# Hybrid gMLP and state-space layer: where the first scalings of the second projection stand on VectorE, and the order of its weight places

## The chip, the cores and the metric

The kernel runs on one core of a Trainium2 chip. A core has a matrix engine (PE), a vector engine (DVE), a scalar engine (ACT), GpSimd (POOL) and SyncE (SP), which here only sends DMAs. Each engine takes its instructions in order, and waits for the others through semaphores. The metric is the device time of one execution in microseconds.

## The reference

One layer on 1024 tokens of width 1024, in float32. The parts around the change:

```
proj = h @ w_in                       # 11296 columns: u, v, z of the gMLP; z, x, B, C, dt of the state space; two gates
y_a = spatial_gating(gelu(gm_u), gelu(gm_v), ...) * silu(gm_z)
y_b = ssd_scan(xh, dt, a, bm, cm)     # 8 groups x 8 chunks of 128 tokens, state carried from chunk to chunk
y_b = y_b + xh * d_skip[:, None]
yz  = (y_b * silu(ssm_z)).reshape(b, s, 8, 256)
y_b = rms_norm(yz, ssm_norm_w)        # root mean square over each group's 256 channels
merged = sigmoid(g_a) * (y_a @ w_proj_a) + sigmoid(g_b) * (y_b @ w_proj_b)
x = x + gate * (merged @ w_out)       # and a last rms_norm over the row
```

## The kernel before

Every large product is made with float32r matmuls of a high and a low part of each operand: high x high, high x low and low x high, three matmuls of 128x128 by 128x512. The kernel has four stages in a row on PE: the input projection; the state-space stage; the second projection, y_b @ w_proj_b; and the output projection.

**The state-space stage** has 32 steps, (group, pair of chunks), written (g,s), in pairs of groups; the last four are (6,2), (7,2), (6,3) and (7,3). A step has three parts. `prep` makes products and transposes on PE (`pc`, `px`); DVE multiplies the decay matrix `dcy` with `pc` (L1183) and scales the transposed input into `xd` and `xe` (L1186). `front` multiplies them (`yi`, and `sp` for the state); DVE adds `sp` to the state `st` (L1236) and forms `y` (L1216). `back` multiplies the state (`yn` in PSUM, eight matmuls of which the last four need the new `st`), DVE scales that by `ea` into `ym` (L1262), and POOL makes y + ym (L1264) and y times z (L1265), which is `yz`. ACT stores `yz` to `yb_d` in device memory. For the root mean square ACT squares `yz` (L1289; for the last halves, `lq`, L1281), POOL adds the two squares (L1293, L1285), PE sums over channels (`pq`), DVE copies that to `cwt` or `tri` (L1305), and it goes through `ms_d` to POOL's power (L1320) and as `rs_d` back to memory. Between the steps PE is filled with matmuls of the first projection, `pma`, which DVE scales into `tha` (L1526) and ACT stores to `mt_d`.

Within this stage each engine's order is written out: `link(key, f)` makes the instructions of `f` stand behind the last linked one of that engine. What is not linked is placed by the scheduler at build time, by its own priorities.

**The second projection** has 56 units, (product, k) for seven products of 2x2 blocks and eight slices of 128 channels, each of twelve matmuls of 128x512; the first product is `p1` (`x0p` to `x3p`). `loads(u)` runs six units ahead and sends, on SP, the tile `rb` (the inverse roots, one for two slices), the row tile `yn` (slice n and half h of y_b from `yb_d`) and the weights: for `p1` raw ones, `p1r`, 128x512. `operands(u)` runs four units ahead: DVE scales `yn` by weight and `rb` (`y_norm`, L1653), ACT and DVE split it into `p1bh` and `p1bl` (L1691, L1692), and the raw weights into `p1a` (L1698, L1699). The first of these loads and operands are issued while the state-space stage still runs. (The name `yn` is used twice: PE's result in `back`, and these row tiles.)

The raw weights of `p1`, and later the gate tiles `tg` and `ma` and `junk`, lie in places that the state-space stage leaves: three each of `xd` and `xe`, two of `ea`. `gate_slot` deals them out in a fixed order of eight. SP's queue is in order too: a load whose place is not yet free holds all loads behind it. All DMAs of SP and ACT share eight semaphores in rotation (DMAHW0 to 7), and each waits until the one before it on its semaphore has landed.

Of the kernel before, what the change touches and what calls it, by code (L numbers as in the profile page):

```python
# [12 lines left out]
ALU = mybir.AluOpType  # L13
# [22 lines left out]
def hybrid_kernel(  # L36
# [7 lines left out]
    V, A, G, PE = nc.vector, nc.scalar, nc.gpsimd, nc.tensor  # L44
# [85 lines left out]
    snw = par2[:, 32:48]  # L130
# [980 lines left out]
    def link(key, f):  # L1111
        if key in last:
            with tc.issue_after(last[key]):
                i = f()
        else:
            i = f()
        last[key] = i.ins
        return i
# [330 lines left out]
    p2r = ps1 = psum = None  # L1449
# [9 lines left out]
    for n, (name, _, _, d1, d2, g) in enumerate(todo):  # L1459
# [11 lines left out]
        if n == len(jobs):  # L1471
# [6 lines left out]
            p2r = p2rpool.__enter__()  # L1478
# [4 lines left out]
        if n + 2 == len(todo):  # L1483
            wspool.__exit__(None, None, None)
            p2xpool = tc.tile_pool(name="p2x", bufs=1, side="right", reuse_waits="tile")
            p2x = p2xpool.__enter__()
# [132 lines left out]
    def slot_tile(name, dt=F32):  # L1619
        tag = room.pop(0)  # L1620
        t = hp.tile([P, 512], dt, name=name, tag=tag)
        tags_of[name] = tag
        return t
# [4 lines left out]
    n_gate = [0]  # L1628

    def gate_slot(name):  # L1630
        n_gate[0] += 1
        pool, tag, b = ((p2x, "xd", 3), (p2x, "xe", 3), (p2r, "ea", 2), (p2x, "xd", 3), (p2x, "xe", 3), (p2x, "xd", 3),
                        (p2x, "xe", 3), (p2r, "ea", 2))[n_gate[0] % 8]
        return pool.tile([P, 512], F32, name=name, tag=tag, bufs=b)


# [4 lines left out]
    yt, rbs = {}, {}  # L1641
# [8 lines left out]

    def y_norm(n, h):
        t = yt[n, h]
        V.scalar_tensor_tensor(t, t, snw[:, n : n + 1], rbs[n // 2, h], op0=ALU.mult, op1=ALU.mult)  # L1653

    units = [(nm, k) for nm in ("p1", "p3", "p6", "p5", "p7", "p2", "p4") for k in range(KT)]
    aops, bops, raws = {}, {}, {}
# [3 lines left out]
    def loads(u):  # L1660

        nm, k = units[u]
        if nm in fresh:
            n, h = fresh[nm]
            y_load(n + k, h)
        aops[u] = t = big(f"{nm}a{k}", F32R).rearrange("p (v c) -> p v c", v=2)
        if nm in WB:
            load(f32(t), wb_d[k][:, WB[nm]])
        else:
            raws[u] = raw = gate_slot(f"{nm}r{k}") if nm == "p1" else slot_tile(f"{nm}r{k}")  # L1670
            n = k if nm == "p1" else KT + k
            load(raw, w_proj_b[n * P : (n + 1) * P, 0:512])

    def operands(u):

        nm, k = units[u]
        if nm in fresh:
            n, h = fresh[nm]
            y_norm(n + k, h)
# [43 lines left out]
    def gate_load(b, h):  # L1723
        hs = slice(h * 512, (h + 1) * 512)
        th, ma = gate_slot(f"tg{b}_{h}"), gate_slot(f"ma{b}_{h}")
        load(th, th_d[(KT + b) * P : (KT + b + 1) * P, hs])
        load(ma, mt_d[b][:, hs])
        gates[b, h] = th, ma
# [109 lines left out]
    for u, (nm, k) in enumerate(units):  # L1838
# [28 lines left out]
        if k == KT - 1:  # L1867
            for j in range(4):
                with tc.high_priority():
                    if nm in ("p1", "p3", "p5"):  # L1870
                        t = slot_tile(f"{nm}_{j}")
# [80 lines left out]
    SPLITS = {"a11": ("t1",), "s1": ("t2",), "s2": ("t3",), "s3": ("t4", "b22"), "a22": ("b21",)}  # L1952
    acc = {"x": banks("ox", "y"), "y": banks("oy", "x")}
    junk = gate_slot("junk")
    for nm, bn, pn, first, t0, c, done in PRODUCTS:
        ps = acc[pn]
# [112 lines left out]
```

## Time and profile before

| | us |
|---|---|
| median of 3 runs | 1365.01 (1363.45 to 1365.26) |
| profiled execution | 1364.88 |
| its span, first to last instruction | 1362.9 |
| PE busy | 1348.8 |
| DVE busy | 1056.7 |
| ACT busy | 800.2 |
| POOL busy | 195.6 |

The profile shows one execution; times in its rows are us from the start of the span. A row of a timeline gives start, duration, engine, line, operation and tiles, the number of instructions that it merges, and in brackets how long the engine had been idle before and what ended that. The profiled execution's own time is 2.0 us longer than the span.

### The profile page before, as it was taken

How to read it: one execution, taken by the hardware profiler on the slowest of the kernel's cores; microseconds unless marked ns; L12 is line 12 of the kernel's file. 1: busy time of each engine (PE TensorE's matmuls, PEld its weight loads, DVE VectorE, ACT ScalarE, POOL GpSimd, SP SyncE). 2: the span in 40 equal slices, each digit the busy share in tenths (PEclk: the TensorE clock that was granted, in tenths of full speed). 3: DMA queues.
4: the chain of work that ended last, by engine and by line, in shares of the span. 5: the costliest groups of instructions: out<-in, count | busy, mean ns of one | idle time of the engine just before them, and what ended most of it. 6: DMA issues, size and time to landing. Idle time of an engine off the chain costs nothing. (4 is left out here: it accounts for less than half of the span.)

```text
span 1362.9 us, 20106 instructions
## 1 busy us (share of the span) xinstructions
PE 1348.8 (99%) x6907; PEld 1115.4 (82%) x6907; DVE 1056.7 (78%) x1731; ACT 800.2 (59%) x1446; POOL 195.6 (14%) x193
## 2 busy tenths in 40 slices
PE   8999999999999999999999999999999999999997
PEld 6688888888888888888888888888888878888886
DVE  4786886787777898688887788458888867959976
ACT  4754666666657665466576655486877734233453
POOL 1000000000000000000000000007898971000002
PEclk9999999999999999999999999999999999999999
DMA  9675444333345667777656866489889868978913
GB/s 284 184 247 140 136 124 124 117 119 121 101 132 155 193 185 230 245 217 245 204 193 192 245 203 185 158 295 307 304 294 315 303 235 289 318 261 319 377 50 124
DMA packets 249577, 288.64 MB, mean 212 GB/s; under 512 B 16860, under 2 KB 196484, under 8 KB 249476
## 3 DMA queue, kind: packets, MB, share of 16 engines
q1 hardware_dynamic: 174868, 203.80, 46.9%
q10 hardware_dynamic: 74544, 83.57, 17.9%
q8 instruction: 54, 0.88, 0.3%
q14 instruction: 47, 0.39, 0.1%
q0 software_dynamic: 64, 0.00, 0.0%
HBM read 199.82 MB, written 87.49 MB: 211 GB/s over the span
## 5 line engine op out<-in xcount | busy, mean ns | idle before, releaser
L1159 POOL TENSOR_SCALAR_AFFINE_SELECT dcy<-dcy 128x1024 f32<-128x1024 f32 x32 | 35.3, 1103 | 787.9 <-DMA yl<-ya_d 744.6
L1167 ACT ACTIVATE dcy<-dcy,nacs 128x128 f32<-128x128 f32 x256 | 78.3, 389 | 2.9 <-POOL dcy L1159 2.3
L1265 POOL TENSOR_TENSOR yz<-y,sl 128x512 f32<-128x512 f32 x32 | 44.7, 1396 | 2.5
L1183 DVE TENSOR_TENSOR dcy<-dcy,pc 128x1024 f32<-128x1024 f32 x32 | 39.0, 1219 | 7.5 <-PE pc L85 5.9
L82 PE MATMUL pma<-yh,wah 128*128 128x512 f32 x128 | 43.1, 418 | 0.0
L82 PE MATMUL pma<-yh,wal 128*128 128x512 f32 x128 | 42.5, 413 | 0.0
L1190 ACT COPY bn<-pc 128x256 f32<-128x256 f32 x32 | 11.9, 371 | 49.6 <-DVE dcy L1183 48.7
L1653 DVE SCALAR_TENSOR_TENSOR yn<-yn,par,rb 128x512 f32<-128x512 f32 x32 | 25.6, 801 | 19.5 <-DMA yn<-yb_d 19.5
L82 PE MATMUL pma<-yl,wah 128*128 128x512 f32 x128 | 40.2, 395 | 0.0
L1155 ACT ACTIVATE ea<-dcy 64x512 f32<-64x512 f32 x64 | 39.8, 622 | 0.4
L1060 ACT ACTIVATE ac<-ac 128x1024 f32<-128x1024 f32 x32 | 34.0, 1061 | 9.2 <-DVE ac L1058 9.0
L1264 POOL TENSOR_TENSOR y<-y,ym 128x512 f32<-128x512 f32 (+1 forms) x32 | 37.0, 1156 | 7.1 <-DVE ym L1262 7.1
L1058 DVE SCALAR_TENSOR_TENSOR ac<-c2x,cwt,ac 128x1023 f32<-128x1023 f32 (+2 forms) x24 | 30.7, 1280 | 8.8 <-ACT ac L1056 8.7
L1058 DVE SCALAR_TENSOR_TENSOR ac<-c2cb,cwt,ac 128x1023 f32<-128x1023 f32 (+2 forms) x24 | 30.7, 1279 | 8.1 <-ACT ac L1056 8.0
L1925 POOL TENSOR_TENSOR r<-r,fnw 128x512 f32<-128x512 f32 x4 | 6.1, 1528 | 206.9 <-ACT junk L1923 206.9
L82 PE MATMUL yi<-dcy,xd 128*64 128x128 f32 x512 | 35.0, 279 | 0.0
L82 PEld LDWEIGHTS yn<-sl,st 128*128 128x128 f32 x224 | 29.8, 191 | 4.0 <-DVE st L1236 1.2
L82 PE MATMUL sp<-xe,bn 128*128 128x256 f32 x112 | 32.7, 409 | 0.0
L82 PEld LDWEIGHTS yi<-dcy,xd 128*64 128x64 f32 x512 | 27.3, 136 | 5.7 <-issue 2.9
L1058 DVE SCALAR_TENSOR_TENSOR ac<-c1cb,cwt,ac 128x1023 f32<-128x1023 f32 (+2 forms) x24 | 30.6, 1277 | 1.3 <-ACT ac L1056 1.3
L82 PE MATMUL yn<-sl,st 128*128 128x128 f32 x224 | 30.5, 275 | 1.0 <-DVE st L1236 1.0
L1022 ACT ACTIVATE vm<-vm,vr 128x128 f32<-128x128 f32 x64 | 25.6, 483 | 9.5 <-DMA vm<-v_d 9.0
(2983 smaller groups left out, 4363.7 us busy)
## 6 DMA issues: line engine op xcount, KB each, us to landing
sl<-s_d SPq DMA_DIRECT2D x32, 768.0 KB, 6.6
s_d<-ac ACTq DMA_DIRECT2D x32, 512.0 KB, 3.3
wb_d<-wbb ACTq DMA_DIRECT2D x32, 512.0 KB, 3.8
dcy<-acs_d SPq DMA_DIRECT2D x32, 512.0 KB, 4.6
av<-in_w_in_dram SPq DMA_DIRECT2D x36, 256.0 KB, 3.3
aw<-in_ada_w_dram SPq DMA_DIRECT2D x16, 512.0 KB, 5.2
wbr<-in_w_proj_b_dram SPq DMA_DIRECT2D x32, 256.0 KB, 4.7
yb_d<-yz ACTq DMA_DIRECT2D x32, 256.0 KB, 5.6
```

What stands on the lines that cost most here:

```text
L82: pin(PE.matmul(acc, l, r, start=first, stop=last))
L1022: A.activation(vn[:, cs], vn[:, cs], AF.Identity, scale=vr[:, 1, ch : ch + 1], bias=vr[:, 2, ch : ch + 1])
L1058: V.scalar_tensor_tensor(ac[:, s:], cc[:, : S - s], conv_wt[:, 3 - s, i : i + 1], ac[:, s:], op0=ALU.mult, op1=ALU.add)
L1060: A.activation(ac, ac, AF.Silu)
L1155: link("A", lambda: A.activation(ea[hh * HD : (hh + 1) * HD], dcy.rearrange("p (j e) i l -> p e j (i l)", e=2)[hh * HD : (hh + 1) * HD, hh ...
L1159: link("G", lambda: G.affine_select(out=d8, in_=d8, compare_op=ALU.is_ge, fill=-1e30, base=0, pattern=[[0, 2 * HPG], [1, P]], channel_mult ...
L1167: link("A", lambda: A.activation(dcy[:, h, i, :], dcy[:, h, i, :], AF.Exp, bias=sub[:, i, h : h + 1]))
L1183: link("V", lambda: V.tensor_tensor(d3, d3, pc[:, 0:256].unsqueeze(1).to_broadcast([P, HPG, 256]), op=ALU.mult))
L1190: link("A", lambda: A.copy(bn, pc[:, 256:512]))
L1264: link("G", lambda: G.tensor_add(y1[:, :, t0:], y1[:, :, t0:], m[:, :, t0:]))
L1265: link("G", lambda: G.tensor_mul(yz, y1, sl[:, 4:6]))
L1653: V.scalar_tensor_tensor(t, t, snw[:, n : n + 1], rbs[n // 2, h], op0=ALU.mult, op1=ALU.mult)
```

## The change

Two edits. The scalings of the first four row tiles (n < 4, first half) are linked: they stand on DVE behind the last linked instruction of the state-space stage. And `gate_slot` deals the eight places in another order: counted from the first call, xe, ea, xd, xe, xd, xe, ea, xd before, and xe, xd, xe, xd, xe, xd, ea, ea now.

```
     def gate_slot(name):
         n_gate[0] += 1
-        pool, tag, b = ((p2x, "xd", 3), (p2x, "xe", 3), (p2r, "ea", 2), (p2x, "xd", 3), (p2x, "xe", 3), (p2x, "xd", 3),
-                        (p2x, "xe", 3), (p2r, "ea", 2))[n_gate[0] % 8]
+        pool, tag, b = ((p2r, "ea", 2), (p2x, "xe", 3), (p2x, "xd", 3), (p2x, "xe", 3), (p2x, "xd", 3), (p2x, "xe", 3),
+                        (p2x, "xd", 3), (p2r, "ea", 2))[n_gate[0] % 8]
...
     def y_norm(n, h):
         t = yt[n, h]
-        V.scalar_tensor_tensor(t, t, snw[:, n : n + 1], rbs[n // 2, h], op0=ALU.mult, op1=ALU.mult)
+        f = lambda: V.scalar_tensor_tensor(t, t, snw[:, n : n + 1], rbs[n // 2, h], op0=ALU.mult, op1=ALU.mult)
+        if n < 4 and h == 0:
+            link("V", f)
+        else:
+            f()
```

PE's, POOL's and SP's instructions stand in the same order as before. DVE at the end of the state-space stage (the first numbers in a name are group and pair of chunks, or the row tile and its half):

```order
 L1216 SCALAR_TENSOR_TENSOR y17_2_10717<-sl7_2_10373,dskt_151,yi7_2_10703 128x256 x2
 L1236 TENSOR_TENSOR st22_8261<-st22_8261,sp7_2_10712 128x256
-L1653 SCALAR_TENSOR_TENSOR yn0_0_10925<-yn0_0_10925,par2_147,rb0_0_10923 128x512
 L1262 TENSOR_TENSOR ym7_2_10749<-yn7_2_10743,ea7_2_10375 128x512
 L1183 TENSOR_TENSOR dcy7_3_10526<-dcy7_3_10526,pc7_3_10754 128x1024
```

The scaling of row tile 0 no longer stands ahead of step (7,2)'s `ym`. Some rows on, still DVE:

```order
-L1653 SCALAR_TENSOR_TENSOR yn1_0_10930<-yn1_0_10930,par2_147,rb0_0_10923 128x512
 L1262 TENSOR_TENSOR ym6_3_10804<-yn6_3_10799,ea6_3_10456 128x512
 L1236 TENSOR_TENSOR st_8258<-st_8258,sp7_3_10819 128x256
 L1216 SCALAR_TENSOR_TENSOR y17_3_10822<-sl7_3_10528,dskt_151,yi7_3_10810 128x256 x2
+L1262 TENSOR_TENSOR ym7_3_10841<-yn7_3_10836,ea7_3_10530 128x512
+L1653 SCALAR_TENSOR_TENSOR yn0_0_10925<-yn0_0_10925,par2_147,rb0_0_10923 128x512
+L1653 SCALAR_TENSOR_TENSOR yn1_0_10930<-yn1_0_10930,par2_147,rb0_0_10923 128x512
 L1653 SCALAR_TENSOR_TENSOR yn2_0_10937<-yn2_0_10937,par2_147,rb2_0_10935 128x512
-L1262 TENSOR_TENSOR ym7_3_10841<-yn7_3_10836,ea7_3_10530 128x512
 L1526 SCALAR_TENSOR_TENSOR tha6_0_10575<-tha6_0_10575,pma6_0_10577 128x512
```

Step (7,3)'s `ym` now stands ahead of the scalings of row tiles 0, 1 and 2, which come together behind it; that of row tile 3 stands one `tha` later. Behind these, DVE's copy of pq(6,1) to `cwt` (L1305) moves from behind the first `p1bl` and `p1a` to ahead of them.

SP's loads of the second projection, before, with the semaphores that each waits for:

```order
L91 DMA p1r1_10933<-in_w_proj_b_dram 128x512 [waits DMAHW4_49,DVE_49,Activation_49]
L91 DMA rb2_0_10935<-rs_d1_59 128x512 [waits DMAHW5_49]
L91 DMA yn2_0_10937<-yb_d2_93 128x512 [waits DMAHW7_49]
L91 DMA p1r2_10940<-in_w_proj_b_dram 128x512 [waits DMAHW0_49]
L91 DMA yn3_0_10949<-yb_d3_94 128x512 [waits DMAHW1_49]
L91 DMA p1r3_10952<-in_w_proj_b_dram 128x512 [waits DMAHW2_49,PE_49]
```

And now:

```order
L91 DMA p1r1_10933<-in_w_proj_b_dram 128x512 [waits DMAHW4_49]
L91 DMA rb2_0_10935<-rs_d1_59 128x512 [waits DMAHW5_49,DVE_49,Activation_49]
L91 DMA yn2_0_10937<-yb_d2_93 128x512 [waits DMAHW6_49]
L91 DMA p1r2_10940<-in_w_proj_b_dram 128x512 [waits DMAHW7_49,DVE_49,PE_49]
L91 DMA yn3_0_10949<-yb_d3_94 128x512 [waits DMAHW0_49,Activation_49]
L91 DMA p1r3_10952<-in_w_proj_b_dram 128x512 [waits DMAHW1_49]
```

`p1r1` had a place of `ea`, and its waits for DVE and ACT were for step (6,3)'s `ym` and `ea`; it now has a place of `xd` that step (7,2) left, and waits only for an earlier DMA. The waits of `rb2` are for step (6,2); `p1r2` waits for `sp` of step (6,3).

## The prediction

> **What bounds the kernel now.** I read the page first (span, busy time of each engine), then the list of PE's waits, then how busy PE is in the stretch behind the change, and last the timelines of PE, VectorE (DVE), POOL, SyncE's queue (SPq) and ScalarE (ACT) around it.
>
> ```profile
> span 1362.9 us, 20106 instructions
> ...
> PE 1348.8 (99%) x6907; PEld 1115.4 (82%) x6907; DVE 1056.7 (78%) x1731; ACT 800.2 (59%) x1446; POOL 195.6 (14%) x193
> ...
> PE yn L82 <- DVE st L1236: 1.0, 1, 1.0
> PE pq L82 <- POOL yz L1293: 0.9, 1, 0.9
> ...
> 1127.00:1350.00 223.00, 222.97 (x984) 184.37 (x983) 183.72 (x301) 84.99 (x160) 10.34 (x8) 1.00 0.71 254
> ```
>
> PE works 99% of the span, so the time can only fall by what PE waits. Two of its few waits lie at the end of the state-space stage, where the change is. From 1127 to 1350 PE is busy for 222.97 of 223.00 us at a granted clock of 1.00: what PE gains before 1127 is carried to the end, as long as its operands come that much sooner too.
>
> PE around the two waits (start, us, work, count; in brackets the idle time before):
>
> ```profile
> 1099.99 1.05 PE L82 MATMUL yn<-sl,st 128*128 128x128 f32 x8
> 1100.88 0.39 PE L82 MATMUL pc<-sl 128*128 128x128 f32 x2
> ...
> 1101.65 0.27 PE L85 MATMUL pc<-ident,sl 128*128 128x128 f32 x1
> ...
> 1103.10 0.70 PE L82 MATMUL sp<-xe,bn 128*128 128x256 f32 x2
> ...
> 1105.48 0.60 PE L82 MATMUL yn<-sl,st 128*128 128x128 f32 x4
> 1107.07 0.71 PE L82 MATMUL yn<-sl,st 128*128 128x128 f32 x4 [0.98 <-DVE st L1236]
> 1107.71 1.09 PE L82 MATMUL yi<-dcy,xd 128*64 128x128 f32 x16
> ...
> 1111.59 1.05 PE L82 MATMUL yn<-sl,st 128*128 128x128 f32 x8
> 1112.40 0.71 PE L82 MATMUL pma<-yh,wal 128*128 128x512 f32 x2
> ...
> 1113.49 0.43 PE L82 MATMUL pq<-yz,ones 128*32 128x128 f32 x8
> 1114.82 0.43 PE L82 MATMUL pq<-yz,ones 128*32 128x128 f32 x8 [0.90 <-POOL yz L1293]
> 1115.18 0.73 PE L82 MATMUL pma<-yl,wah 128*128 128x512 f32 x2
> ...
> 1122.21 0.42 PE L82 MATMUL pq<-lq,ones 128*32 128x128 f32 x8
> ...
> 1125.06 0.42 PE L82 MATMUL pq<-lq,ones 128*32 128x128 f32 x8
> ...
> 1126.91 0.39 PE L1718 MATMUL x0p<-p1bh,p1a 128*128 128x512 f32 x1
> ```
>
> The first wait costs more than its bracket: eight yn matmuls take 0.81 us from start to next start when undisturbed (1111.59 to 1112.40), here 2.23 (1105.48 to 1107.71). The difference is 1.42, or 1.34 against the yn group at 1099.99, which takes 0.89 (0.11 a matmul) when state-space work follows (1100.88), as it does here; I take 1.35. The second is 1114.82 - 1113.49 less the 0.36 that such a group takes (1114.82 to 1115.18): 0.97.
>
> Why DVE and POOL are late there:
>
> ```profile
> 1103.01 0.75 DVE L1653 SCALAR_TENSOR_TENSOR yn<-yn,par,rb 128x512 f32<-128x512 f32 x1 [3.48 <-DMA yn<-yb_d]
> 1103.68 0.68 DVE L1262 TENSOR_TENSOR ym<-yn,ea 128x512 f32<-128x512 f32 x1
> 1104.28 1.21 DVE L1183 TENSOR_TENSOR dcy<-dcy,pc 128x1024 f32<-128x1024 f32 x1
> ...
> 1106.61 0.41 DVE L1236 TENSOR_TENSOR st<-st,sp 128x256 f32<-128x256 f32 x1
> ...
> 1107.72 1.71 DVE L1653 SCALAR_TENSOR_TENSOR yn<-yn,par,rb 128x512 f32<-128x512 f32 x1
> ...
> 1116.15 0.75 DVE L1653 SCALAR_TENSOR_TENSOR yn<-yn,par,rb 128x512 f32<-128x512 f32 x1 [5.02 <-DMA yn<-yb_d]
> 1116.82 0.68 DVE L1262 TENSOR_TENSOR ym<-yn,ea 128x512 f32<-128x512 f32 x1
> ...
> 1124.03 1.38 DVE L1692 TENSOR_TENSOR p1bl<-yn,p1bh 128x512 fp32r<-128x512 f32 x1 [0.72 <-ACT p1bh L1691]
> 1125.33 0.68 DVE L1699 TENSOR_TENSOR p1a<-p1r,p1a 128x512 fp32r<-128x512 f32 x1
> ```
> ```profile
> 1099.61 1.64 POOL L1320 TENSOR_TENSOR ssq<-ssq,nhalf 128x8 f32<-128x8 f32 x1
> 1104.44 1.29 POOL L1264 TENSOR_TENSOR y<-y,ym 128x512 f32<-128x512 f32 x1 [3.19 <-DVE ym L1262]
> ...
> 1107.61 1.27 POOL L1293 TENSOR_TENSOR yz<-yz 128x512 f32<-128x512 f32 x1
> 1108.84 2.10 POOL L1320 TENSOR_TENSOR ssq<-ssq,nhalf 128x8 f32<-128x8 f32 x1
> 1110.90 1.28 POOL L1264 TENSOR_TENSOR y<-y,ym 128x512 f32<-128x512 f32 x1
> ...
> 1113.51 1.26 POOL L1293 TENSOR_TENSOR yz<-yz 128x512 f32<-128x512 f32 x1
> ...
> 1123.57 1.29 POOL L1285 TENSOR_TENSOR lq<-lq,lq 128x512 f32<-128x512 f32 x1 [1.74 <-ACT lq L1281]
> ```
> ```profile
> 1097.21 0.42 SPq L91 DMA_DIRECT2D yn<-yb_d  x1
> ...
> 1110.09 0.33 SPq L91 DMA_DIRECT2D p1r<-in_w_proj_b_dram  x1
> ...
> 1110.95 0.42 SPq L91 DMA_DIRECT2D yn<-yb_d  x1
> ...
> 1122.34 1.15 ACT L1281 ACTIVATE lq<-yz 128x512 f32<-128x512 f32 x2 [5.19 <-DMA mt_d<-tha]
> ```
>
> DVE runs in order. The scaling of row 0 stands ahead of step (7,2)'s ym and waits 3.48 us for its load; ym, dcy, xd, xe and st behind it are late, and PE waits for st. The same ym starts POOL's chain late (3.19 idle), which then runs without a break to the sum at 1113.51, and PE waits for that one. Later the scaling of row 2 waits 5.02 us ahead of step (7,3)'s ym, because SPq sent its load only at 1110.95, behind p1r1, whose place was free only after step (6,3)'s ym.
>
> **The change part by part.** No work is added or removed: the same 32 scalings, the same loads. Four scalings move on DVE, and p1r1 to p1r7 change places.
>
> *Scalings, first wait.* Without the scaling ahead, ym of (7,2) starts when PE's group of 1099.99 ends, about 1101.07. dcy then needs the transposes of 1101.65: it starts at 1102.0 instead of 1104.28, and st 2.33 us behind it as now (1106.61 - 1104.28), at 1104.33. Its input sp ends at 1103.80, so nothing holds it. st ends at 1104.74; PE needs it at 1105.48 + 4 x 0.11 = 1105.92. Margin 1.2 us: the whole 1.35 goes.
>
> *Scalings, second wait.* POOL's first y starts at 1101.83 instead of 1104.44, and its rows keep their distances: the power at 1108.84 - 2.61 = 1106.23, done by 1107.87 with the 1.64 of the row at 1099.61 (1108.33 with the 2.10 here). ym of (6,3) is ready by 1107.2. From the next y to the end of the sum are 3.87 us (1110.90 to 1114.77): 1111.74 to 1112.20. PE comes there at 1113.49 - 1.35 + 0.36 = 1112.50. The 0.97 goes too, with 0.3 to 0.8 us in hand.
>
> *Places.* p1r1 no longer waits for (6,3)'s ym, so SPq goes on at about 1098.7. The loads of rb2 and row 2 are then sent some 11 us sooner; at the 5.8 us from send to use of row 0 (1097.21 to 1103.01) they land near 1106, well before DVE reaches them at 1111.9. p1r2 to p1r5 now wait for matmuls of (6,3) and (7,3), p1r6 and p1r7 for the last ea's; these are needed much later. The gate tiles that use the same eight places later still come eight slots apart. By itself all this costs and brings nothing on PE; it removes the 5.02 us of DVE.
>
> *What is late next.* PE then wants everything from 1115 on 2.32 us sooner: the sums lq by 1119.89 and 1122.74, x0p's operands from 1124.59. ym of (7,3) starts at PE's 1111.59 - 1.35 + 1.08 = 1111.32 instead of 1116.82, 5.5 us sooner, and POOL's last y with it. But now three scalings (0.75 each) stand between it and tha, cwt and tri, on which ACT's in-order queue hangs ahead of lq. The bounds: if DVE runs them unhindered, tri is done at 1116.8, ACT squares lq at 1117.4 and the last sum ends near 1120. If each scaling takes turns with a POOL row, 1.29 + 0.55 us a turn, tri comes at 1119.1, lq's squares (1.15) at 1120.2 and the sum ends at 1122.6. Both are before 1122.74. x0p's third matmul needs p1a's low part, which ends at 1126.01 for a use at 1127.37 now; it is wanted by 1125.05 and, behind lq in ACT, comes between 1122 and 1124.7. So I book nothing here, with 0.2 to 3 us of cover.
>
> *Sum.* 1.35 + 0.97 = 2.32 us off the profiled execution's 1364.88 gives 1362.56. That execution lies 0.13 below the median of 1365.01, so by that it would be 1362.7; with the lowest run at 1363.45 the median stands at the high end, and I say **1362.6**. The bounds of the gain: 1.9 by the brackets alone (0.98 + 0.90), 2.4 with 1.42 for the first.
>
> **Rivals.**
>
> *DVE and POOL take turns, and it costs PE.* The scaling at 1107.72 took 1.71 us instead of 0.75: it ended at 1109.43, 0.55 behind the end of POOL's row at 1107.61 (1108.88), and POOL's next one took 2.10 instead of 1.64. So where both work in SBUF alone they go one after the other, and the change puts three scalings just where POOL has its last y and yz. If scalings of rows 4 and 5 also come ahead of the last lq sum, it ends 2 x 0.55 later, near 1123.7, PE waits 0.9 us there, and the time is 1363.5. Against it: the unhindered order leaves 2.7 us. Chance 0.17. The Trainium skill states this as a rule (SBUF — State Buffer, "SBUF: two separate sides"): the port pair of the two engines is an exclusive lock for the whole instruction, and a VectorE op with two SBUF inputs takes it. By that rule turns are certain and the rival decides by their order; the trace agrees, with 1.71 against 0.75.
>
> *x0p's operands don't come sooner.* They have 1.36 us in hand now (1126.01 to 1127.37). If ACT's queue, held by its stores, kept them there, only 1.36 would be left: 1363.5. For it: lq waits 5.19 us in ACT's queue now. Against it: what it waits for moves 2 to 5 us. Chance 0.10.
>
> *No change: another wait in their place.* If st or the POOL sum stayed late by something that the scaling only covered, 0 to 0.4 us would be left: 1364.8. I find no such row; the rows behind the scaling follow without a gap. Chance 0.08.
>
> *Slower.* DVE now has cwt of pq(6,1) ahead of the first p1bl, and cwt overwrites a tile whose store ACT has sent some time near 1119. Until that store lands, all operands of x0p wait. The nearest price is the 5.8 us of a load: 1124.8, with p1bl and p1a's low part behind it (1.3 us) PE would lose 1.0. If it lands after about 1128.8, 10 us after sending, the kernel is slower by 0.2% (2.7 us lost beyond the 2.32): 1367.8. Chance 0.04.
>
> **How the numbers follow.** Forecast 0.61 and the rivals 0.17, 0.10, 0.08 and 0.04. 0.2% is 2.7 us, about what a measurement of this kernel can tell from no change; the runs shown spread by 1.8 (1363.45 to 1365.26). The forecast gains 2.3 to 2.4, just inside that; with the spread of a median of a few runs about half of its cases, 0.31, come out as faster by over 0.2%. The other half, and all of the partial rivals, are within it: 0.65. Slower: 0.04. The range goes from 1361.6 (gain 2.4 and a low median) to 1364.4 (gain 0.9 and a high one, so the partial rivals are in, most of "no change" and the slower one out).
>
> **What would show it.** DVE's idle times of 3.48 and 5.02 ahead of L1653 gone; the four scalings behind the last ym (L1262); both PE waits gone from the list; p1r1 sent near 1098.7; x0p's first matmul at 1124.6 instead of 1126.91; PE busy without a gap behind it. Wrong would be: a new PE wait for lq's sum, for p1bl or p1a, or x0p starting later than 1125.5.

## The result

| | before | changed |
|---|---|---|
| median, us (22 runs each, same chip) | 1364.23 (1362.22 to 1366.0) | 1361.80 (1360.9 to 1364.56) |
| ratio of the runs | | 0.9986, 95% interval 0.998 to 0.9992 |
| profiled execution, us | 1364.88 | 1362.27 |
| its span | 1362.9 | 1360.4 |

By the medians the changed kernel is 2.4 us (0.18%) faster; by the ratio, which is not the quotient of the medians, it is 0.14% (1.9 us), with an interval of 1.1 to 2.7 us. The forecast was 1362.6, with a gain of 2.3 to 2.4. The page of the changed kernel, its list of PE's waits (engine, tile and line, who is waited for: us in total, times, longest), and a window over what follows x0p's start:

```profile
span 1360.4 us, 20108 instructions
...
PE 1347.0 (99%) x6907; PEld 1114.4 (82%) x6907; DVE 1056.1 (78%) x1731; ACT 800.4 (59%) x1446; POOL 196.1 (14%) x193
```
```profile
PE acc L82 <- DVE b11h L306: 1.5, 1, 1.5
...
PE oy L1914 <- DVE wlt L1803: 0.3, 1, 0.3
```
```profile
1124.10:1347.00 222.90, 222.59 (x982) 183.85 (x981) 184.74 (x302) 84.69 (x159) 9.83 (x8) 1.00 0.70 251
```

Both waits at the end of the state-space stage (`yn` for `st`, `pq` for `yz`) are gone from the list. What is left of it lies elsewhere; the 0.3 for `wlt` is new, in the output projection. PE's timeline where the waits were:

```profile
1099.50 1.05 PE L82 MATMUL yn<-sl,st 128*128 128x128 f32 x8
...
1104.99 1.05 PE L82 MATMUL yn<-sl,st 128*128 128x128 f32 x8
1105.98 1.09 PE L82 MATMUL yi<-dcy,xd 128*64 128x128 f32 x16
...
1111.75 0.64 PE L82 MATMUL pq<-yz,ones 128*32 128x128 f32 x16
1112.33 0.50 PE L82 MATMUL pma<-yl,wah 128*128 128x512 f32 x1
...
1122.24 0.42 PE L82 MATMUL pq<-lq,ones 128*32 128x128 f32 x8
...
1124.10 0.39 PE L1722 MATMUL x0p<-p1bh,p1a 128*128 128x512 f32 x1
...
1124.55 0.48 PE L1722 MATMUL x0p<-p1bh,p1a 128*128 128x512 f32 x1
1124.87 0.40 PE L1722 MATMUL x1p<-p1bh,p1a 128*128 128x512 f32 x1
```

All eight `yn` matmuls run in one group, and the two `pq` groups have become one row of sixteen. The comparison can be made within one execution, by a stopwatch that starts with step (7,2)'s `yn` group and stops with x0p's first matmul: 1126.91 - 1099.99 = 26.92 us before, 1124.10 - 1099.50 = 24.60 now, 2.32 less. The other 0.49 of x0p's earlier start was there already at the start of the stretch, and 0.31 is given back behind it (the span is 2.5 shorter). This **stretch** is used below, since whole runs of one kernel spread by 3 us and more.

DVE and POOL in the same place:

```profile
1100.59 0.69 DVE L1262 TENSOR_TENSOR ym<-yn,ea 128x512 f32<-128x512 f32 x1 [1.55 <-PE yn L82]
...
1103.87 0.41 DVE L1236 TENSOR_TENSOR st<-st,sp 128x256 f32<-128x256 f32 x1
...
1111.55 4.13 DVE L1653 SCALAR_TENSOR_TENSOR yn<-yn,par,rb 128x512 f32<-128x512 f32 x3
1115.60 0.67 DVE L1526 SCALAR_TENSOR_TENSOR tha<-tha,pma 128x512 f32<-128x512 f32 x1
...
1118.10 0.27 DVE L1305 TENSOR_SCALAR tri<-pq 128x128 f32<-128x128 f32 x1
...
1122.99 0.29 DVE L1305 TENSOR_SCALAR cwt<-pq 128x128 f32<-128x128 f32 x1 [3.29 <-PE pq L82]
...
1123.80 0.68 DVE L1703 TENSOR_TENSOR p1a<-p1r,p1a 128x512 fp32r<-128x512 f32 x1
```
```profile
1110.00 1.28 POOL L1293 TENSOR_TENSOR yz<-yz 128x512 f32<-128x512 f32 x1
1111.71 1.72 POOL L1264 TENSOR_TENSOR y<-y,ym 128x512 f32<-128x512 f32 x1 [0.43 <-DVE ym L1262]
1113.51 1.63 POOL L1265 TENSOR_TENSOR yz<-y,sl 128x512 f32<-128x512 f32 x1
1115.09 1.74 POOL L1285 TENSOR_TENSOR lq<-lq,lq 128x512 f32<-128x512 f32 x1
1120.79 1.29 POOL L1285 TENSOR_TENSOR lq<-lq,lq 128x512 f32<-128x512 f32 x1 [3.96 <-ACT lq L1281]
```

DVE's idle times of 3.48 and 5.02 us for row tiles are gone: `ym` waits for PE's `yn`, as it should, and `st` is done 1.1 us before PE needs it at 1104.99 + 4 x 0.11. The POOL sum ends at 1111.28, ahead of PE's 1111.75. What was left to cover is nearly used up: the last `lq` sum ends at 1122.08 for PE at 1122.24, and the low part of `p1a` at 1124.48 for x0p's third matmul, which is held up by 0.09 (the next one starts 0.32 behind it, 1124.55 to 1124.87, instead of 0.23).

### The profile page after: what moved, and what is told of

Read it like the earlier page. It is cut to its first block, busy times and chain, and to the rows that moved or that the text cites. A ratio compares the mean times of both kernels' runs of the same rounds, so it can differ in the third digit from the quotient of the medians.

```text
span 1360.4 us, 20108 instructions
## 1 busy us (share of the span) xinstructions
PE 1347.0 (99%) x6907; PEld 1114.4 (82%) x6907; DVE 1056.1 (78%) x1731; ACT 800.4 (59%) x1446; POOL 196.1 (14%) x193
## 4 chain that ended last, share of the span: by engine, by line
PE 93%; POOL 3%; DMA 1%; issue 1%; ACT 1%; DVE 1%; SPq 0%; POOLq 0%; DVEq 0%; ACTq 0%
PE xcb L585 6%; PE xz L585 6%; PE xuz L585 6%; PE xx L585 6%; PE xg L585 6%; PE pma L82 5%; PE ox L1914 3%; PE yuz L585 3%; PE yx L585 3%; PE ycb L585 3%; PE yp L1722 3%; PE yz L585 3%; PE vx L990 3%; PE yg L585 3%; PE oy L1914 2%; PE x0p L1722 2%
## 5 line engine op out<-in xcount | busy, mean ns | idle before, releaser
L1262 DVE TENSOR_TENSOR ym<-yn,ea 128x512 f32<-128x512 f32 (+1 forms) x32 | 19.9, 621 | 18.2 <-PE yn L82 18.0
```

## The experiments

The theories of the first set. **A**, that of the prediction: row 0's scaling ahead of (7,2)'s `ym` made both waits, and the places bring PE nothing. **B**: what counts is SP's queue, held behind `p1r1`'s place. Three sets ran on three chips, each kernel in five rounds beside the kernel before on the same chip. The ratios differ from the quotients of the medians by up to 0.0006.

| kernel | set | median, us | before, us | ratio (95% interval) | stretch, us |
|---|---|---|---|---|---|
| both edits | 1 | 1365.13 | 1366.93 | 0.9988 (0.9979 to 0.9997) | 24.59 |
| links alone | 1 | 1368.40 | 1366.93 | 1.0012 (1.0004 to 1.0021) | 26.59 |
| places alone | 1 | 1367.51 | 1366.93 | 1.0005 (0.9996 to 1.0014) | 27.00 |
| row 0 linked alone | 1 | 1366.75 | 1366.93 | 1.0000 (0.9991 to 1.0009) | 25.35 |
| own tile for pq(6,1) | 2 | 1362.95 | 1364.03 | 0.9992 (0.9980 to 1.0005) | 24.77 |
| links, place of p1r1 only | 2 | 1362.48 | 1364.03 | 0.9989 (0.9977 to 1.0001) | 24.62 |
| links, small weight loads | 2 | 1362.22 | 1364.03 | 0.9983 (0.9972 to 0.9994) | 24.60 |
| before, no scalings | 2 | 1363.27 | 1364.03 | 0.9991 (0.9979 to 1.0002) | 25.19 |
| before again | 3 | 1363.76 | 1363.44 | 1.0002 (0.9993 to 1.0011) | 26.58 |
| links alone again | 3 | 1362.55 | 1363.44 | 0.9994 (0.9985 to 1.0003) | 24.82 |
| both edits again | 3 | 1361.55 | 1363.44 | 0.9986 (0.9977 to 0.9995) | 24.60 |
| both, no scalings | 3 | 1361.17 | 1363.44 | 0.9989 (0.9981 to 0.9998) | 24.60 |

**Both edits**, as a control in the first set:

> The changed kernel once more, on the chip of the runs beside it. Theory A (the scaling of row 0 ahead of step (7,2)'s ym caused both PE waits): 2.0 to 2.4 us below the kernel before, ratio 0.9985. Theory B (SP's queue behind p1r1's place caused the loss): the same.

Measured: 1.8 us faster, both waits gone, the same stretch as in the first profile (1102.88 to 1127.47).

**Links alone**, with the places of before:

```
-        pool, tag, b = ((p2r, "ea", 2), (p2x, "xe", 3), (p2x, "xd", 3), (p2x, "xe", 3), (p2x, "xd", 3), (p2x, "xe", 3),
-                        (p2x, "xd", 3), (p2r, "ea", 2))[n_gate[0] % 8]
+        pool, tag, b = ((p2x, "xd", 3), (p2x, "xe", 3), (p2r, "ea", 2), (p2x, "xd", 3), (p2x, "xe", 3), (p2x, "xd", 3),
+                        (p2x, "xe", 3), (p2r, "ea", 2))[n_gate[0] % 8]
```

> The scalings of rows 0 to 3 behind the last ym, the places of before. Theory A: both PE waits (0.98 and 0.90) are gone, 2.0 to 2.4 us below before, like the changed kernel within 0.4. SP still stands behind p1r1 until step (6,3)'s ym, now near 1107; rows 2 and 3 are sent near 1108 and land near 1113, about when DVE comes to row 2. Theory B: the late rows hold DVE ahead of tha and ACT's stores, so that PE waits for lq's sum or for x0p's operands instead, and no more than 1 us is gained.

Measured: 1.5 us slower. Theory A holds in its first half, since the old waits are gone, and falls in its second: without the places a new wait stands in PE's way, 10 us later. PE, then SP's load of row 4, then ACT with its queue of stores (ACTq):

```profile
1128.06 0.43 PE L82 MATMUL pq<-lq,ones 128*32 128x128 f32 x8 [1.92 <-POOL lq L1285]
...
1129.91 0.40 PE L1722 MATMUL x0p<-p1bh,p1a 128*128 128x512 f32 x1
```
```profile
1117.21 0.32 SPq L91 DMA_DIRECT2D yn<-yb_d  x1
```
```profile
1123.75 0.33 ACTq L1528 DMA_DIRECT2D mt_d<-tha  x1
...
1124.98 0.48 ACTq L1306 DMA_DIRECT2D ms_d<-tri  x1
1125.51 1.15 ACT L1281 ACTIVATE lq<-yz 128x512 f32<-128x512 f32 x2 [9.60 <-DMA yb_d<-yz]
```

The second store of `tha` and that of `cwt` stand behind two stores of `yz` here, before they stood ahead of them; the changed kernel has the same order on ACT as the links alone, so that doesn't set the two apart. Nor was DVE late: it had `tri` ready 18.4 us after the stopwatch's start (1121.76 - 1103.32), 0.4 sooner than with both edits. But the store of `tri` left at 21.7 instead of 19.5, and `lq`'s squares stand behind it in ACT's order: 22.2 instead of 20.1. What the stores wait for is seen in the program's order:

```
SP    p1r3   128x512 [waits DMAHW2, PE]
SP    rb4    128x512 [waits DMAHW3]
SP    yn4    128x512 [waits DMAHW5, DVE, PE]
SP    p1r4   128x512 [waits DMAHW7]
ACT   mt_d6<-tha6_0  [waits DMAHW2, DVE]
ACT   yb_d14<-yz7_2  [waits DMAHW3, POOL]
ACT   mt_d6<-tha6_1  [waits DMAHW5, DVE]
ACT   ms_d7<-tri     [waits DMAHW7, DVE]
```

Each of these stores takes the semaphore that one of SP's loads had before it, and so must wait until that load has landed. With the places of before, SP is held behind `p1r1` until step (6,3)'s `ym` is done, and then sends its loads in a heap: row 4, for one, which the second store of `tha` has to wait for, was sent at 1117.21, and that store left at 1123.75. The trace also keeps when each semaphore rose, and that shows the hold: `p1r3`, `rb4`, row 4 and `p1r4` landed at 1120.68, 1122.23, 1123.67 and 1124.90, and the four stores above left at 1120.76, 1122.30, 1123.75 and 1124.98, each 0.07 or 0.08 us behind its load, though what they store had been ready 0.7 to 3.4 us earlier. In the changed kernel's first profile the DMAs that these four stores wait for had landed 4.0 to 5.1 us before the stores left.

**Places alone**: `y_norm` as before, the new order in `gate_slot`.

> The new places, the scalings where they were. Theory A: row 0's scaling still waits about 3.5 us ahead of step (7,2)'s ym, both PE waits stay at 0.98 and 0.90, the 5.02 us of DVE ahead of row 2 go, and the time is that of before within 0.4 us (ratio 0.9997 to 1.0003). Theory B: 1.5 to 2.3 us below before.

Measured: no difference that can be told, and both waits are there:

```profile
PE pq L82 <- POOL yz L1293: 1.3, 1, 1.3
...
PE yn L82 <- DVE st L1236: 0.7, 1, 0.7
```

The places are not quite alone in this run: with rows 2 and 3 loaded sooner, the scheduler put row 2's scaling ahead of step (7,3)'s `st` and row 3's ahead of its `ym`. So the second wait, 1.3 instead of 0.9, is not the places' own; that the places don't remove the first wait stands, as row 0's scaling is still ahead of (7,2)'s `ym`.

**Only row 0 linked**, places of before (`if n < 1 and h == 0`):

> Only row 0's scaling behind the last ym; rows 1 to 3 and the places as before. Theory A, in its narrow form that the one scaling did it: both PE waits gone, 1.9 to 2.4 us below before. Rival: the scaling of row 1, which took 1.71 us ahead of step (6,3)'s ym beside POOL, holds POOL's chain by itself; then the first PE wait goes and the second stays with 0.5 to 0.97, and 1.3 to 1.8 us are gained.

Measured: no difference that can be told. The first wait is gone, but the squares of `lq` start 20.9 us after the stopwatch's start, between both edits (20.1) and links alone (22.2), and PE waits 0.6 us for the sums `lq` and 0.3 for `yz`. The scalings of rows 1 and 2 are still ahead of (6,3)'s and (7,3)'s `ym`. In its profile the stretch is 1.2 to 1.6 us shorter than in the two profiles of the kernel before (26.92 and 26.58), of which the medians show nothing; that is left open.

So in the times of this set neither edit gains by itself, and both together do. The second set asked why. **C**: the heap of loads lands late, and ACT's stores, which share the semaphores, wait for it. **D**: the linked scalings themselves, in turns with POOL, hold `tha`, `cwt` and `tri`.

**Links, and only p1r1's place changed** (`p1r1` and `p1r2` change places against the order of before):

```
-        ((p2x, "xd", 3), (p2x, "xe", 3), (p2r, "ea", 2), (p2x, "xd", 3), (p2x, "xe", 3), ...
+        ((p2x, "xd", 3), (p2x, "xe", 3), (p2x, "xd", 3), (p2r, "ea", 2), (p2x, "xe", 3), ...
```

> Scalings linked, and only p1r1 and p1r2 change places against the order of before: p1r1 gets the place of xd, p1r2 the place of ea that is free only after step (6,3)'s ym. rb2 and row 2 are then sent some 10 us sooner; row 3 and all behind it still wait on SP's queue. Theory C (the loads behind the held one go out in a heap, land 6 us after sending, and ScalarE's stores, which share the eight DMA semaphores, wait for them): three loads of sixteen fewer in the heap, the store of tha leaves 1 to 2 us sooner than with the links alone, and between half and all of that kernel's loss goes: 1.7 us faster to 0.3 us slower than the kernel before. Rival A (only row 2 and its scaling matter): the whole gain, 1.7 to 2.4 us faster, and no PE wait for the sums lq. Rival D (the three linked scalings, taking turns with POOL, hold tha, cwt and tri, and the places do nothing): 1.2 us or more slower, as with the links alone.

Measured: the stretch of both edits, 1.5 us faster in the median (the interval just reaches one). SP sends `p1r1`, `rb2` and row 2 at 1098.20 to 1099.14 and is held behind `p1r2` until 1106.80. Three loads fewer in the heap were enough; that also fits theory A's version here (only row 2 matters), so this run alone does not tell C from A. The first set's links alone do: there the third scaling, that of row 2, was as early by the stopwatch as with both edits to within 0.1 us (14.51 and 14.40), and PE waited 1.92 us all the same.

**Links, places of before, small weight loads**: same queue, same semaphores, fewer bytes.

```
-            load(raw, w_proj_b[n * P : (n + 1) * P, 0:512])
+            c = 64 if nm == "p1" and 2 <= k <= 5 else 512
+            load(raw[:, 0:c], w_proj_b[n * P : (n + 1) * P, 0:c])
```

> Scalings linked, places of before, but the raw weights p1r2 to p1r5 are loaded with 64 of their 512 columns and their operands repeat these (the result is not the reference's). Queue, order and semaphores stay as with the links alone; only the bytes in the heap shrink by 0.9 MB. Theory C: p1r3, whose semaphore the store of tha needs, lands 2 us or more sooner, PE's wait of 1.9 us for the last sum lq falls under 0.5, and the time is 1 to 2.2 us below the kernel before. Rival D (turns on DVE): it stays about 1.2 us or more slower than before.

Measured: the whole gain, with rows 2 and 3 sent as late as with the links alone (row 2 at 1108.42, 9.15 us behind the `yn` start; 9.35 with the links alone) and rows 4 and 5 some 1.1 us sooner. `p1r3` landed at 15.1 us by the stopwatch instead of 17.4, and the loads that the four stores wait for had landed 1.0 to 2.3 us before these left. Besides the bytes, and the operands made of them, only one thing differs: the place of the copy of pq(6,1) to `cwt` on DVE, which ran at 1120.81, behind the store of `tri` (1118.60). That speaks against A's version and D. But no run of the links alone stood beside it in this set, and the third set shows that these can come close to the same by themselves; so by its time it supports C and does not prove it.

**The kernel before without the scalings** of row tiles 0 to 3, first half:

> The kernel before, places as before, without the scalings of row tiles 0 to 3 in their first half (left out, so the result is not the reference's). DVE then has no scaling ahead of the last steps, nor any behind them. Theory C: both PE waits go, but SP's queue is held as before, ScalarE's stores and the squares lq stay late, PE waits for the last sum lq or for x0p's operands, and the time is 0.5 us faster to 1.8 us slower than before. Rival D (the linked scalings themselves cost the gain): the whole gain, 1.7 to 2.4 us faster, without any new PE wait.

Measured: 0.76 us faster in the median, with an interval that reaches one, 1.4 to 1.7 in the stretch, and a wait of 0.5 for the last `lq`. That speaks against D, which had no new wait: none of these scalings is in the way, and ACT is late all the same. DVE copies `cwt` at 1115.60, and its store leaves 4 us behind that. The DMA before it on its semaphore was a store of `yz` in the heap, which landed at 1119.66; the store of `tri`, at 1122.60, followed the landing of `p1r4` at 1122.52:

```profile
1119.74 0.50 ACTq L1306 DMA_DIRECT2D ms_d<-cwt  x1
...
1123.14 1.15 ACT L1281 ACTIVATE lq<-yz 128x512 f32<-128x512 f32 x2 [7.52 <-DMA ms_d<-cwt]
```

**pq(6,1) copied to a tile of its own**, in the changed kernel:

```
-            pq, row = rows_bank[0](f"pq{g}_{q}"), (cwt, tri)[g % 2]
+            pq, row = rows_bank[0](f"pq{g}_{q}"), par if late and g == NG - 2 else (cwt, tri)[g % 2]
```

> The changed kernel, but the copy of pq(6,1) goes to a tile of its own instead of cwt, so that it no longer overwrites a tile whose store may still be under way. In the profile of the changed kernel DVE idles 3.3 us ahead of that copy, though its PE sum had ended 3 us before. Theory: it waits for the store of cwt to land, and this costs PE only about 0.1 us at x0p's third matmul. Expected: DVE's idle time there falls from 3.3 us to under 1.5 (then p1bh's row on ScalarE sets p1bl), and the time is that of the changed kernel: 1.6 to 2.4 us below the kernel before. Rival: that store is what holds x0p's operands and more than x0p hangs on it: then 0.5 us or more faster than the changed kernel.

Measured: the copy follows its matmuls at once, and x0p's third matmul is no longer late, but nothing is gained over the changed kernel. The median is 1.1 us below before, short of the 1.6 expected, with an interval from 2.7 us faster to 0.7 slower:

```profile
1119.84 0.29 DVE L1305 TENSOR_SCALAR par<-pq 128x128 f32<-128x128 f32 x1 [0.19 <-PE pq L82]
1121.49 1.39 DVE L1696 TENSOR_TENSOR p1bl<-yn,p1bh 128x512 fp32r<-128x512 f32 x1 [1.36 <-ACT p1bh L1695]
```

The 3.29 us that the changed kernel's profile puts down to PE's `pq` were for the most part the wait for the store of the old `cwt`, which landed at 1122.52: the prediction's "slower" rival. It cost PE 0.09 us.

The third set repeated what mattered.

> The kernel before once more, as a gauge: how far two sets of runs of one kernel differ, and how long the stretch from step (7,2)'s yn matmuls to x0p's first matmul is on PE in another execution. Expected: 26.9 us as in the profile before (1099.99 to 1126.91), and a time within 0.1% of the other runs of before. If the stretch differs by more than 0.2 us, the comparison by stretches falls.

Measured: the two sets of runs agree within 0.02%, but the stretch is 26.58, 0.34 shorter than in the first profile. By what was written down, the comparison by stretches falls: where PE's work hangs on loads, the stretch moves by 0.3 us and more from one execution to the next. What is left of it is the changed kernel's, which stood at 24.59 to 24.60 in three executions; its distance to the two profiles of before is 2.0 to 2.3.

> Links alone once more. In its first profile the stretch from yn to x0p was 26.59 us, 0.33 shorter than before, and yet its runs were 1.5 us longer. Theory C (the loss that the places avert is all in that stretch): stretch 26.4 to 26.8 again, time 1 us faster to 0.7 slower than before; the 1.5 us were chance. Rival (links alone cost something outside the stretch, too): again 1 us or more slower, and the span less the stretch is 1 us longer than that of the kernel before.

Measured: 0.9 us faster in the median, which may be no difference; a stretch of 24.82, and so neither what theory C gave in numbers nor the rival. The same program had 26.59 before. The last two columns of a window are the mean DMA share and GB/s. For the links alone in the first and in the third set, the 14 us from SP's release on in two windows of 7; then the second of these windows (14.3 to 21.3 us by the stopwatch) with small loads, and with both edits in the first profile:

```profile
1110.60:1117.60 7.00, 7.00 (x52) 5.46 (x49) 4.05 (x6) 1.15 (x2) 6.42 (x6) 1.00 0.52 151
1117.60:1124.60 7.00, 7.00 (x37) 5.36 (x37) 4.88 (x8) 0.00 (x0) 3.05 (x2) 1.00 1.03 351
```
```profile
1105.94:1112.94 7.00, 7.00 (x52) 5.46 (x49) 4.05 (x6) 1.15 (x2) 6.41 (x6) 1.00 0.79 217
1112.94:1119.94 7.00, 7.00 (x38) 5.36 (x37) 5.59 (x9) 0.88 (x2) 3.05 (x2) 1.00 1.03 389
```
```profile
1113.55:1120.55 7.00, 7.00 (x37) 5.36 (x37) 5.48 (x9) 1.41 (x3) 3.23 (x3) 1.00 0.90 304
```
```profile
1113.80:1120.80 7.00, 7.00 (x38) 5.35 (x37) 5.90 (x9) 1.25 (x3) 3.04 (x3) 1.00 0.73 255
```

With the links alone the DMA engines are full (1.03) just when ACT wants to store; with fewer bytes or with the places they are not (0.90, 0.73). But they are as full in the execution that lost little. The two differ in how fast the heap starts: 151 GB/s in the first 7 us of the one, 217 in the other. `p1r3`, `rb4`, row 4 and `p1r4` then landed 1.1 to 2.7 us sooner by the stopwatch, ahead of the stores by 0.1 to 0.8 us, and DVE had `tri` ready at 18.4 us in both. By the stopwatch the store of `tri` left 2.0 us sooner (1118.34 - 1098.66 = 19.7 against 21.7), the squares of `lq` started at 20.4 instead of 22.2, and PE waited 0.16 us for the last sum instead of 1.92:

```profile
1118.34 0.67 ACTq L1306 DMA_DIRECT2D ms_d<-tri  x1
1119.06 1.15 ACT L1281 ACTIVATE lq<-yz 128x512 f32<-128x512 f32 x2 [7.29 <-DMA yb_d<-yz]
```

One program, the same instructions and the same scalings, and loads that moved at another speed: with the landings this shows C, more than any of the edits. The profiled execution was also the fastest of the eleven (1360.99; the median is 1362.55), so the usual stretch probably lies above 24.82. The 1.5 us of loss in the first set are thus not all explained: of the 3.3 us between links alone and both edits there, 2.0 lie in the stretch. The spans of the two profiles differ by 2.6: 0.4 ahead of the stretch, 2.0 in it and 0.2 behind it; the rest of the 3.3 is between executions. Why the heap moved more slowly in the one execution, and what the 0.4 ahead are, stays open.

> The changed kernel once more beside these. Expected: stretch 24.6 us, 2.3 shorter than before, and a time 1.7 to 2.4 us below the kernel before.

Measured: 1.9 us faster, stretch 24.60.

**The changed kernel without the scalings** of row tiles 0 to 3, first half:

> The changed kernel without the scalings of row tiles 0 to 3 in their first half (left out, so the result is not the reference's); places as in the changed kernel. Tells what the turns of DVE and POOL (three scalings in 4.13 us) still cost. Theory: nothing, since they are within the cover: tha, cwt, tri and the last sum lq come 1 to 4 us sooner, the stretch stays at 24.5 to 24.6 us, the time is that of the changed kernel within 0.4 us. Rival (turns cost PE): the stretch or the rest gets shorter by 0.3 us or more.

Measured: the last `lq` sum starts at 1119.16 for PE at 1124.06, 3.6 us of cover instead of 0.16, and PE is no sooner: 24.60, and 0.4 us less in the median, with intervals that overlap. The turns of DVE and POOL cost cover and no time that can be told. POOL and PE:

```profile
1119.16 1.29 POOL L1285 TENSOR_TENSOR lq<-lq,lq 128x512 f32<-128x512 f32 x1 [1.28 <-ACT lq L1281]
```
```profile
1124.06 0.42 PE L82 MATMUL pq<-lq,ones 128*32 128x128 f32 x8
```

## Why the prediction came out, and the step in it that did not

*The sum.* Forecast 1362.6, measured 1361.8; the gain in the stretch is 2.32 us, the number of the sum. Two errors cancel in it. The first wait gave 2.23 - 0.99 = 1.24 instead of 1.35: eight `yn` matmuls ahead of `yi` take 0.99 us (1104.99 to 1105.98), not 0.89. The second gave 1.69 - 0.58 = 1.11 instead of 0.97: from the first `pq` to the next `pma` were 1.69 us (1113.49 to 1115.18), and sixteen `pq` matmuls in one go take 0.58 (1111.75 to 1112.33), not twice 0.36. Together they make 2.35, of which the stretch shows 2.32. The medians fell by 2.43, but the interval of the ratio allows 1.1 to 2.7 us, so their agreement with the sum to 0.1 is in part luck; the 0.8 that is left to the forecast is its choice of the high end of the three runs of before: the 22 runs beside the changed kernel have a median of 1364.23, 0.8 below 1365.01.

*Times in the stretch.* Shifted by the 0.49, `st` was due at 1103.84 and started at 1103.87; the last `lq` sum, with turns, was due to end at 1122.1 and ended at 1122.08; `p1r1` was due near 1098.2 and was sent at 1098.24, and rows 0 to 2 were there when DVE came to them.

*What failed* is the step *Places*: "By itself all this costs and brings nothing on PE". Places alone do bring nothing, but the sentence let the whole gain rest on the scalings, and the links alone gave from 1.5 us of loss to 0.9 of gain. The places are what lets the gain through: they send `p1r1`, `rb2` and row 2 some 8 to 10 us sooner than the links alone do (`p1r1` 1.3 us ahead of the stopwatch's start instead of 7.3 behind it), so that what ACT's last stores wait for has landed 4 us and more before them. The rival "x0p's operands don't come sooner", with ACT's queue held by its stores, named that mechanism but gave it no source; it is what the slower execution of the links alone shows.

*The rivals.* Turns: they came about, at three scalings in 4.13 us, and took all but 0.16 us of the cover without costing PE. No change: no. Slower by the store of `cwt`: the wait was there, its copy came at 1122.99 (due at 1124.3 with the load's price), and it cost 0.09 us instead of 1.0.

## What to carry to other kernels

When a wait goes, ask of every store and load in the next 10 us whose semaphore it takes and whether those in front will have landed: an in-order load queue that is freed late sends a heap, and the heap can hold stores of another engine that have no data in common with it. Two edits of which neither gains surely alone can still both be needed; a two-by-two of them shows it, where the sum of single effects would not. In such a table look at the order that each kernel was built with: a scheduler can move more than the edit. A stopwatch between two instructions of the busy engine in one profile tells 0.3 us apart where whole runs spread by 3, but only where nothing in between waits for a DMA.

## What the hardware showed beside this

DVE and POOL slowed each other on rows of 128x512 in SBUF: three scalings took 4.13 us, the first 0.74 and the two behind it 1.77 and 1.78 (0.75 alone), while POOL's rows took 1.72, 1.63 and 1.74 (1.28 to 1.30 alone). They end in turns: each of the two later scalings ends 0.54 us behind a row of POOL's (1113.43 to 1113.97, 1115.14 to 1115.68), and each of POOL's rows 1.14 to 1.17 behind a scaling. The Trainium skill (SBUF — State Buffer, "SBUF: two separate sides") tells of an exclusive lock for the whole instruction; these rows agree with it, with 0.1 to 0.2 us of each row outside the turn.

An instruction that the change does not touch, POOL's `dcy` mask, took 3.5 us instead of 1.09 in five of the fourteen profiled executions (all four of the first set, and "before, no scalings"), and PE then waited 2.4 us for the state. POOL with both edits, in the first set and in the first profile:

```profile
915.94 3.52 POOL L1159 TENSOR_SCALAR_AFFINE_SELECT dcy<-dcy 128x1024 f32<-128x1024 f32 x1 [18.62 <-ACT ea L1155]
```
```profile
914.74 1.09 POOL L1159 TENSOR_SCALAR_AFFINE_SELECT dcy<-dcy 128x1024 f32<-128x1024 f32 x1 [18.62 <-ACT ea L1155]
```

That is as much as the whole effect studied here, and may be one reason for the spread of the runs; its cause was not looked into.
